# A gated MLP on one Trainium2 core: seven-product up tiles for 28 of 44 tiles, with part of VectorE's work moved to GpSimd

## The chip, the core and the metric

The kernel runs on one core of a Trainium2 chip. The core has TensorE (PE; its weight loads are shown as PEld), VectorE (DVE), ScalarE (ACT), GpSimd (POOL) and SyncE (SP), which issues DMAs here. The metric is the device time of one execution in microseconds (us); less is better.

## What is computed

One layer of an encoder in float32: attention in two head groups, an output projection, and a gated MLP with a convolution of width 3 over the positions of the gate branch. The change concerns the MLP:

```
def conv_glu(x, w_gate, w_up, conv_w, conv_b, w_down):
    g = x @ w_gate
    u = x @ w_up
    pad = CONV_W // 2
    gp = jnp.pad(g, ((0, 0), (pad, pad), (0, 0)))
    gc = conv_b
    for i in range(CONV_W):
        gc = gc + conv_w[i] * gp[:, i:i + L]
    return (jax.nn.silu(gc) * u) @ w_down
```

The model width is 2048 (16 blocks of 128 rows, `KC`), the hidden width 5632 (44 tiles of 128, `FC`), and 256 positions count at the end; 258 are carried where the convolution needs its neighbours.

## The kernel before

*Numbers in two parts.* TensorE multiplies in a reduced float32 form (`fp32r`). To keep precision every operand is split: a high part `whi` (ScalarE's copy into that form) and a low part `wlo = raw - whi` (VectorE's subtraction). A product then takes three matmuls (high by high, high by low, low by high). Each weight that is loaded (`raw`) therefore costs a ScalarE and a VectorE instruction over all its columns: `split_hi`, `split_lo`, line L251 (ScalarE) and L255 (VectorE's two-operand instructions). There are four `whi` and four `wlo` buffers, so at most four pieces of 1024 columns stand ready or in use.

*Kinds of tile.* A **gate tile** is 16 blocks of three matmuls over 258 columns (`mm3`, L734 to L736), an ordinary **up tile** 16 blocks of one matmul over 512 columns (high by both parts of x) and one over 256 (`mm2`, L2056 and L2057). Four up tiles that form a **quad** are done another way, by a scheme with seven products of 2 x 2 blocks in place of eight (`RowPair`, `scheme_products`, L291): for each of 8 pairs of row blocks, 7 products of three matmuls over 256 columns. It needs sums of the four weight quarters (`weight_sums`: one VectorE instruction over 512 columns and two over 256, each of which uses the result of the one before), which are split like weights, and sums `S` of the blocks of x, which lie ready in `near` buffers (or are loaded). So a pair has 1792 columns to split and not 1024. At a quad's end `quad_out` and `seven` combine the products (7 VectorE instructions that read a PSUM bank), eight transposes on TensorE (L297) turn the result, and `quad_value` multiplies it by the gate.

*The gate branch.* `gated` scales the product, `convolved` applies the three taps: the first on ScalarE (L251), the second and the third on VectorE (L263), then ScalarE's silu. `finish_value` splits the product of gate and up tile into `act`, and `pair_sums`/`value_sums` make, for every two tiles, the sums that the down products need: four VectorE instructions over 128 columns, then two splits (`split_plain`).

*Order.* `QUADS = (4, 10, 16, 22, 28)` names each quad's first tile. The list `work` is the order of pieces on TensorE: for each quad its 16 pieces are interleaved with those of the gate tiles (and of the ordinary gate and up tiles up to the next quad). From tile 34 on the rest is mixed with the products of the down projection. The queues of all engines are written out beforehand by a planner (`Flow`): every instruction is a `yield` of an engine and a cost in ns, the planner picks the one that can start first, and each engine then runs its list in that order. `ACT`, `TT` and `STT` (VectorE), `PTT` (GpSimd, L279) and `MM` are such helpers. `made` is the pool of buffers for weight sums; in the MLP it holds one (`more_raw`) until later buffers join it. `near_to(g)` says for how many quads the sums `S` of pair g stay in an `act` buffer that its values do not need yet; `ev_far` tells when it is free.

Of the kernel before, what the change touches and what calls it, by code (L numbers as in the profile page):

```python
# [9 lines left out]
F32 = mybir.dt.float32  # L10
F32R = mybir.dt.float32r
# [4 lines left out]
P = 128  # L16
# [30 lines left out]
ST = SF // P  # L47
SL = 1024
SM = SF - SL
QUADS = (4, 10, 16, 22, 28)  # L50
MID = 34


def near_to(g):

    return sum(f <= FC - KC + 2 * g for f in (*QUADS, MID)[1:])


# [160 lines left out]
def encoder_block(ctx: ExitStack, tc: tile.TileContext, io):  # L219
# [57 lines left out]
    def PTT(out, a, b, op):  # L277
        yield "pool", 90 + (2.7 if fl.cur.t < 4e5 else 3.9) * size(out)
        nc.gpsimd.tensor_tensor(out, a, b, op)  # L279

    def cost(l, r):
        n, m = size(r), l.shape[-1]
        if r.dtype != F32R:
            return max(1.69 * n, 3.33 * m, 50)
        return 0.445 * n + 3 if n >= 256 else max(0.84 * n, 0.84 * m, 27)

    def MM(items):

# [193 lines left out]
    for w, f in enumerate(QUADS):  # L482

        g, end = f // 2, (*QUADS, MID)[w + 1] // 2
        rest = tile_pair("gate", g) + tile_pair("gate", g + 1)
        for i in range(g + 2, end):
            rest += tile_pair("gate", i) + tile_pair("up", i)
        scheme = []
        for i in range(KC // 2):
            r = RowPair(io["w_up_s"][w][i], i, PW // 4, "up")  # L490
            r.first, r.last, r.quad = i == 0, i == KC // 2 - 1, f
            r.near = w < near_to(i)
            r.last_near = w + 1 == near_to(i)
            scheme += [(p, "scheme", r, 0) for p in r.pieces]
        lead, tail = 3, 2
        middle = rest[lead : len(rest) - tail]
        work += rest[:lead]
        for i, u in enumerate(scheme):
            a, b = (j * len(middle) // len(scheme) for j in (i, i + 1))
            work += [u] + middle[a:b]  # L500
        work += rest[len(rest) - tail :]
# [127 lines left out]
    def weight_sums(r):  # L629
        yield r.loaded  # L630
        q = r.q
        if r.wide:
            if r.mode == "both":
                yield r.summed[0]
                r.at["more"] = yield from one(made)
            else:
                yield r.first_loaded
                r.at["two"], r.at["more"] = yield made, 2
            low, up, t, m = (r.at[k] for k in ("lower", "upper", "two", "more"))
            if r.mode == "both":  # L640
# [12 lines left out]
            return  # L653
        t = r.at["sums"] = yield from one(made)
        raw = r.at["raw"]
        if r.mode == "third":
            yield from TT(t[:, :q], raw[:, :q], raw[:, q : 2 * q], ALU.add)
            yield from TT(t[:, q : 2 * q], t[:, :q], raw[:, 3 * q :], ALU.add)
            yield from TT(t[:, 2 * q : 3 * q], t[:, :q], raw[:, 2 * q : 3 * q], ALU.subtract)
            fl.set(r.summed[0])  # L660
        else:
            yield from TT(t[:, : 2 * q], raw[:, q : 3 * q], raw[:, : 2 * q], ALU.add)
            fl.set(r.summed[0])
            yield from TT(t[:, 2 * q : 3 * q], raw[:, 2 * q : 3 * q], t[:, :q], ALU.add)
            yield from TT(t[:, 3 * q :], t[:, 2 * q : 3 * q], raw[:, 3 * q :], ALU.add)
        fl.set(r.summed[1])
        r.used("raw")

# [61 lines left out]

    def mm3(ps, xhi, xlo, start, stop):
        whi, wlo = yield from block()
        yield "pe", 3 * (0.445 * size(xhi) + 3)
        nc.tensor.matmul(ps, whi, xhi, start=start, stop=False)  # L734
        nc.tensor.matmul(ps, whi, xlo, start=False, stop=False)  # L735
        nc.tensor.matmul(ps, wlo, xhi, start=False, stop=stop)  # L736
        used()
# [416 lines left out]
    sum_b = apool.tile([P, NT], F32, name="sum_b")  # L1154
    ev_sum_a, ev_sum_b = Event(), Event()

    def split_plain(hi, lo, src):
        yield from ACT(hi, src, AF.Copy)
        yield from TT(lo, src, hi.bitcast(F32), ALU.subtract)

# [736 lines left out]
    def mlp_buffers():  # L1897

        nonlocal act, mts, mpool
        yield ev_s2t  # L1900
        yield ev_resT
        actx.close()
        mpool = ctx.enter_context(tc.tile_pool(name="mpool", bufs=1))
        act = mpool.tile([P, FC, 2, SEQ], F32R, name="act")
        mt_rows[:] = tiles(mpool, 3, [P, 4 * NT], "mt")
        mts = Slots([t[:, i * NT : (i + 1) * NT] for t in mt_rows for i in range(4)])
        for t in tiles(mpool, 2, [P, PW], "sin"):
            fl.put(s_parts, t)
        for t in tiles(mpool, 1, [P, PW], "more_raw"):
            fl.put(made, t)  # L1910
        for b in banks[4:]:
            fl.put(acc, b)
        for i in range(KC // 2):
            f = FC - KC + 2 * i
            near[i] = act[:, f : f + 2].rearrange("p f i t -> p (f i t)").bitcast(F32)
        fl.set(ev_mlp)
        for i, (dst, saved) in enumerate(saved_sums["up"][:EARLY]):
            yield saved
            yield "sp", 600
            load(near[i], dst, ev_near[i], nc.sync)  # L1920
# [12 lines left out]
    def convolved(f, gs):  # L1933
        gc = yield from one(mts)
        g_ = gc[:, :SEQ]
        yield from ACT(
            g_, gs[:, 1 : 1 + SEQ], AF.Identity, scale=vec("conv0", f), bias=vec("conv_b", f)
        )
        yield from STT(g_, gs[:, :SEQ], vec("conv1", f), g_, ALU.mult, ALU.add)
        yield from STT(  # L1940
            gc[:, 1:SEQ], gs[:, : SEQ - 1], vec("conv2", f), gc[:, 1:SEQ], ALU.mult, ALU.add
        )
        yield from ACT(gs[:, :SEQ], g_, AF.Silu)
        fl.put(mts, gc)
        gates[f] = gs
        fl.set(ev_gate[f])
# [11 lines left out]
    def finish_value(f, u):  # L1958
        fl.put(mts, gates[f])
        u_ = u[:, :SEQ]  # L1960
        if f >= FC - KC:
            yield ev_far[(f - FC + KC) // 2]
        yield from ACT(act[:, f, 0, :], u_, AF.Copy)
        yield from TT(act[:, f, 1, :], u_, act[:, f, 0, :].bitcast(F32), ALU.subtract)
# [12 lines left out]
    def value_sums(dst, saved, a, b, place=None):  # L1977

        (A11, A21), (A12, A22) = ((t[:, :P], t[:, P:SEQ]) for t in (a, b))

# [71 lines left out]
    def mm2(ps, x, n, start, stop):  # L2052

        whi, wlo = yield from block()
        yield "pe", 347
        nc.tensor.matmul(ps, whi, x, start=start, stop=False)  # L2056
        nc.tensor.matmul(ps[:, :n], wlo, x[:, 0, :], start=False, stop=stop)  # L2057
        used()
# [4 lines left out]
    def mlp_weights():  # L2063
        pss, f = [], 0
        for p, kind, which, q in work:
# [15 lines left out]
            else:  # L2081
                if f == 0:
                    ps = yield from one(acc)
                for _ in range(p.n // P):
                    yield ev_act[f]
                    if which < KC - ST - 1:
                        yield from mm2(ps, act[:, f], SEQ, f == 0, f == FC - 1)
                    else:
                        yield from mm3(
                            ps[:, :SEQ], act[:, f, 0, :], act[:, f, 1, :], f == 0, f == FC - 1  # L2090
                        )
                    f += 1
                if f == FC:
# [29 lines left out]
    def scheme_products(p, r):  # L2123
# [5 lines left out]
        for i, n in enumerate(p.products):  # L2129
            if r.first:  # L2130
                yield from sums7_bank(r, n)
            if n in (1, 2, 4):
                k, h = {1: (0, 0), 2: (1, 0), 4: (1, 1)}[n]
                k += 2 * r.g
                A = hl[k] if r.of == "up" else act[:, k]
                a = [A[:, j, h * P : (h + 1) * P] for j in range(2)]
            else:
                yield r.ev_S
# [16 lines left out]
        if p is r.pieces[-1]:  # L2155
# [14 lines left out]
            if r.last:  # L2170
# [301 lines left out]
```

## Time and profile before

| | |
|---|---|
| runs | 1103.39, 1103.25, 1102.38 us; median 1103.25 |
| span of the profiled execution | 1102.0 us |
| its own time beside the span | the page gives no other; the span is 1.25 us under the median |
| TensorE, VectorE, ScalarE, GpSimd busy | 99%, 92%, 68%, 11% of the span |
| granted TensorE clock | 0.999 |
| attention and output projection | from 0 to about 400 us, the last of it beside the first gate tiles |
| gate and up tiles | from about 390 to 921 us |
| rest of the down products | to the end |

In the profile, a line of a group reads: source line, engine, operation, output<-inputs, partitions x elements and type, count | busy us, mean ns | idle us of the engine just before, and what ended it. In an order of time: start us, us from the start to the end, engine and instruction, count when alike ones are merged. Instructions of one engine overlap a little, so the distance of two starts says more than a duration.

### The profile page before, as it was taken

The page shows a single profiled execution, that of the slowest core. Times are in us where ns is not written, and L with a number is a line of the kernel's source. Part 1 is how long each engine was busy: PE and PEld are TensorE (multiplying, and loading weights), DVE is VectorE, ACT ScalarE, POOL GpSimd, SP SyncE. Part 2 cuts the span into 40 slices and gives each one's busy share as a digit, 9 for nine tenths or more (in the row PEclk, how much of TensorE's full clock was granted, in tenths as well). Part 3 has the DMA queues.
Part 4 walks back from the last instruction along what each step waited for, and adds up shares of the span by engine and source line. Part 5 has one row for each costly group of instructions (what it writes and reads, how often), then busy time and mean ns, then how long its engine had stood idle before and what let it go on. Part 6 is the DMA issues. An engine that isn't in the chain of part 4 may idle for free.

```text
span 1102.0 us, 22408 instructions
## 1 busy us (share of the span) xinstructions
PE 1094.0 (99%) x8164; PEld 1046.5 (95%) x8164; DVE 1015.0 (92%) x1935; ACT 751.1 (68%) x1507; POOL 120.8 (11%) x199
## 2 busy tenths in 40 slices
PE   9999999999999999999999999999999999999998
PEld 9999999999999999999999999999999999888887
DVE  8969887988878989999999999999999989999997
ACT  8688978888646776656666666665666656566663
POOL 3211222232443400000000000000000000000001
PEclk9999999999999999999999999999999999999999
DMA  9765678567877778655666656758788878699891
GB/s 327 253 230 176 197 218 236 149 203 182 255 207 208 229 256 324 215 193 192 224 221 209 225 192 237 262 193 285 264 299 287 292 237 322 205 320 336 302 331 45
DMA packets 82166, 262.72 MB, mean 238 GB/s; under 512 B 9224, under 2 KB 13320, under 8 KB 82056
## 3 DMA queue, kind: packets, MB, share of 16 engines
q1 hardware_dynamic: 78600, 252.38, 66.0%
q0 software_dynamic: 3168, 8.65, 5.2%
q8 instruction: 64, 1.05, 0.4%
q14 instruction: 46, 0.38, 0.1%
q10 hardware_dynamic: 288, 0.27, 0.1%
HBM read 243.82 MB, written 34.08 MB: 252 GB/s over the span
## 4 chain that ended last, share of the span: by engine, by line
PE 87%; ACT 5%; DVE 4%; DMA 2%; issue 1%; SPq 0%; POOL 0%; DVEq 0%; ACTq 0%; POOLq 0%
PE bank L291 27%; PE bank L734 14%; PE bank L735 14%; PE bank L736 14%; PE bank L2056 11%; PE bank L2057 6%; PE bank L297 2%; ACT whi L251 1%; DVE wlo L255 1%; DVE scr L263 1%; ACT scr L251 1%; DMA scr<-scr 1%; ACT qraw L251 0%; DMA early<-in_w_down_s 0%; DMA raw<-in_w_cq 0%
## 5 line engine op out<-in xcount | busy, mean ns | idle before, releaser
L251 ACT ACTIVATE whi<-raw 128x512 fp32r<-128x512 f32 (+2 forms) x493 | 354.1, 738 | 158.5 <-PE bank L735 54.6
L255 DVE TENSOR_TENSOR wlo<-raw,whi 128x512 fp32r<-128x512 f32 (+2 forms) x493 | 408.0, 848 | 30.7 <-ACT whi L251 29.8
L734 PE MATMUL bank<-hl,whi 128*128 128x258 f32 (+1 forms) x1208 | 347.8, 288 | 0.1
L735 PE MATMUL bank<-hl,whi 128*128 128x258 f32 (+1 forms) x1208 | 343.7, 285 | 0.0
L736 PE MATMUL bank<-hl,wlo 128*128 128x258 f32 (+1 forms) x1208 | 343.1, 284 | 0.2 <-DVE wlo L255 0.2
L736 PEld LDWEIGHTS bank<-hl,wlo 128*128 128x128 f32 x1208 | 229.7, 190 | 0.6 <-DVE wlo L255 0.4
L735 PEld LDWEIGHTS bank<-hl,whi 128*128 128x128 f32 x1208 | 229.3, 190 | 0.1
L734 PEld LDWEIGHTS bank<-hl,whi 128*128 128x128 f32 x1208 | 228.2, 189 | 0.8 <-ACT scr L251 0.3
L291 PE MATMUL bank<-whi,act 128*128 128x256 f32 (+1 forms) x574 | 143.5, 302 | 0.0
L2056 PE MATMUL bank<-hl,whi 128*128 128x512 f32 x384 | 136.6, 395 | 0.0
L2057 PE MATMUL bank<-hl,wlo 128*128 128x256 f32 x384 | 107.7, 280 | 0.0
L291 PEld LDWEIGHTS bank<-whi,act 128*128 128x128 f32 x574 | 100.2, 189 | 5.2
L251 ACT ACTIVATE whi<-more_raw 128x1024 fp32r<-128x1024 f32 x69 | 71.8, 1040 | 42.7 <-DVE more_raw L255 22.7
L291 PE MATMUL bank<-wlo,act 128*128 128x256 f32 (+1 forms) x287 | 86.8, 302 | 0.0
L2056 PEld LDWEIGHTS bank<-hl,whi 128*128 128x128 f32 x384 | 72.1, 188 | 14.9
L255 DVE TENSOR_TENSOR wlo<-more_raw,whi 128x1024 fp32r<-128x1024 f32 x69 | 82.6, 1196 | 3.2 <-ACT whi L251 3.1
L279 POOL TENSOR_TENSOR halves<-halves,resT 128x256 f32<-128x256 f32 x4 | 3.0, 784 | 703.9 <-ACT halves L251 703.9
L2057 PEld LDWEIGHTS bank<-hl,wlo 128*128 128x128 f32 x384 | 72.4, 188 | 0.0
L291 PE MATMUL bank<-whi,sin 128*128 128x256 f32 (+1 forms) x248 | 69.0, 325 | 0.0
L251 ACT ACTIVATE whi<-halves 128x1024 fp32r<-128x1024 f32 (+2 forms) x57 | 52.2, 936 | 22.4 <-PE bank L291 7.5
L255 DVE TENSOR_TENSOR wlo<-halves,whi 128x1024 fp32r<-128x1024 f32 (+2 forms) x57 | 60.4, 1074 | 0.5 <-ACT whi L251 0.3
L291 PEld LDWEIGHTS bank<-wlo,act 128*128 128x128 f32 x287 | 54.3, 189 | 2.2
(323 smaller groups left out, 2216.1 us busy)
## 6 DMA issues: line engine op xcount, KB each, us to landing
raw<-in_w_gate SPq DMA_DIRECT2D x88, 512.0 KB, 5.1
raw<-in_w_in SPq DMA_DIRECT2D x52, 512.0 KB, 4.5
raw<-in_w_up SPq DMA_DIRECT2D x48, 512.0 KB, 4.5
raw<-in_w_up_s SPq DMA_DIRECT2D x40, 512.0 KB, 4.4
raw<-in_w_out SPq DMA_DIRECT2D x32, 512.0 KB, 5.1
sin<-s_down SPq DMA_DIRECT2D x28, 512.0 KB, 6.5
raw<-in_w_down_m SPq DMA_DIRECT2D x21, 512.0 KB, 5.4
s_down<-sums SPq DMA_DIRECT2D x20, 512.0 KB, 6.5
```

What stands on the lines that cost most here:

```text
L251: nc.scalar.activation(out, in_, f, **kw)
L255: nc.vector.tensor_tensor(out, a, b, op)
L263: nc.vector.scalar_tensor_tensor(out, a, s, b, op0, op1)
L279: nc.gpsimd.tensor_tensor(out, a, b, op)
L291: nc.tensor.matmul(o, l, r, start=start, stop=stop)
L297: nc.tensor.transpose(o, i, ident[:n, :n])
L734: nc.tensor.matmul(ps, whi, xhi, start=start, stop=False)
L735: nc.tensor.matmul(ps, whi, xlo, start=False, stop=False)
L736: nc.tensor.matmul(ps, wlo, xhi, start=False, stop=stop)
L2056: nc.tensor.matmul(ps, whi, x, start=start, stop=False)
L2057: nc.tensor.matmul(ps[:, :n], wlo, x[:, 0, :], start=False, stop=stop)
```

## The change

Quads start every four tiles (seven of them); between two quads there are then no ordinary gate and up tiles, and only after the last quad do two follow. In `weight_sums` the two 256-wide sums go to GpSimd for the up weights. In `convolved` the third tap is ScalarE's product and GpSimd's addition. In `pair_sums` the two low parts are GpSimd's for the first 18 of 22 pairs. The sums `S` of pair 2 no longer lie in `act`: they are loaded for each quad, and the 4 KB a partition so saved are a second buffer for weight sums (`more_sums`) until the last quad, then the values of tiles 32 and 33 (`act_two`). The planner's TensorE costs change from `0.445 * n + 3` to `stream(n)`, and the pieces ahead and behind in a quad's order from 3 and 2 to 2 and 1.

```
-QUADS = (4, 10, 16, 22, 28)
+QUADS = (4, 8, 12, 16, 20, 24, 28)
...
+SUMS_IN = 2
 def near_to(g):
+    if g == SUMS_IN:
+        return 0
     return sum(f <= FC - KC + 2 * g for f in (*QUADS, MID)[1:])
...
+    def stream(n):
+        return n / 2.4 + 0.436 * -(-n // 16) + 4.7
...
-        return 0.445 * n + 3 if n >= 256 else max(0.84 * n, 0.84 * m, 27)
+        return stream(n) if n >= 256 else max(0.84 * n, 0.84 * m, 27)
...
-        lead, tail = 3, 2
+        lead, tail = 2, 1
...
             yield from TT(t[:, : 2 * q], raw[:, q : 3 * q], raw[:, : 2 * q], ALU.add)
             fl.set(r.summed[0])
-            yield from TT(t[:, 2 * q : 3 * q], raw[:, 2 * q : 3 * q], t[:, :q], ALU.add)
-            yield from TT(t[:, 3 * q :], t[:, 2 * q : 3 * q], raw[:, 3 * q :], ALU.add)
+            op = PTT if r.of == "up" else TT
+            yield from op(t[:, 2 * q : 3 * q], raw[:, 2 * q : 3 * q], t[:, :q], ALU.add)
+            yield from op(t[:, 3 * q :], t[:, 2 * q : 3 * q], raw[:, 3 * q :], ALU.add)
...
-        yield "pe", 3 * (0.445 * size(xhi) + 3)
+        yield "pe", 3 * stream(size(xhi))
...
-    def split_plain(hi, lo, src):
+    def split_plain(hi, lo, src, TT=TT):
...
-        act = mpool.tile([P, FC, 2, SEQ], F32R, name="act")
+        tile_of = mpool.tile([P, FC - 2, 2, SEQ], F32R, name="act")
+        f = FC - KC + 2 * SUMS_IN
+        act = [tile_of[:, i - 2 * (i > f)] for i in range(FC)]
...
+        near[SUMS_IN] = mpool.tile([P, PW], F32, tag="act_two", name="more_sums")
+        fl.put(made, near[SUMS_IN])
...
-        yield from STT(
-            gc[:, 1:SEQ], gs[:, : SEQ - 1], vec("conv2", f), gc[:, 1:SEQ], ALU.mult, ALU.add
-        )
+        yield from ACT(gs[:, : SEQ - 1], gs[:, : SEQ - 1], AF.Copy, scale=vec("conv2", f))
+        yield from PTT(gc[:, 1:SEQ], gc[:, 1:SEQ], gs[:, : SEQ - 1], ALU.add)
...
-        yield from value_sums(*saved_sums["down"][g], *(t[:, :SEQ] for t in pair))
+        op = PTT if g < LAST - 3 else TT
+        yield from value_sums(*saved_sums["down"][g], *(t[:, :SEQ] for t in pair), TT=op)
...
-            yield from split_plain(hl_[:, i], hl_[:, 2 + i], t)
+            yield from split_plain(hl_[:, i], hl_[:, 2 + i], t, TT)
...
-        yield "pe", 347
+        yield "pe", stream(2 * SEQ) + stream(SEQ)
...
                     fl.spawn(quad_out(r.quad, r.order, P7, dict(sum_banks)))
+                    if r.quad == QUADS[-1]:
+                        fl.spawn(sums_out())
+
+    def sums_out():
+        for t in (yield made, 2):
+            if t is not near[SUMS_IN]:
+                fl.put(made, t)
+        f = FC - KC + 2 * SUMS_IN
+        t = mpool.tile([P, 2, 2, SEQ], F32R, tag="act_two", name="act_two")
+        act[f : f + 2] = [t[:, i] for i in range(2)]
+        fl.set(ev_far[SUMS_IN])
```

More of the change, by code (lines that the diff above doesn't have):

```diff
@@ L1914, in mlp_buffers @@
             f = FC - KC + 2 * i
-            near[i] = act[:, f : f + 2].rearrange("p f i t -> p (f i t)").bitcast(F32)
+            t = tile_of[:, f - 2 * (i > SUMS_IN) :][:, :2]
+            near[i] = t.rearrange("p f i t -> p (f i t)").bitcast(F32)
+        near[SUMS_IN] = mpool.tile([P, PW], F32, tag="act_two", name="more_sums")
+        fl.put(made, near[SUMS_IN])
         fl.set(ev_mlp)
         for i, (dst, saved) in enumerate(saved_sums["up"][:EARLY]):
+            if i == SUMS_IN:
+                continue
             yield saved
@@ L1962, in finish_value @@
             yield ev_far[(f - FC + KC) // 2]
-        yield from ACT(act[:, f, 0, :], u_, AF.Copy)
-        yield from TT(act[:, f, 1, :], u_, act[:, f, 0, :].bitcast(F32), ALU.subtract)
+        yield from ACT(act[f][:, 0, :], u_, AF.Copy)
+        yield from TT(act[f][:, 1, :], u_, act[f][:, 0, :].bitcast(F32), ALU.subtract)
         fl.set(ev_act[f])
@@ L1976, in encoder_block, with value_sums @@
     values, last_S = {}, {g: ([], Event()) for g in (LAST - 1, LAST)}
-    def value_sums(dst, saved, a, b, place=None):
+    def value_sums(dst, saved, a, b, place=None, TT=TT):
         (A11, A21), (A12, A22) = ((t[:, :P], t[:, P:SEQ]) for t in (a, b))
@@ L2086, in mlp_weights @@
                     if which < KC - ST - 1:
-                        yield from mm2(ps, act[:, f], SEQ, f == 0, f == FC - 1)
+                        yield from mm2(ps, act[f], SEQ, f == 0, f == FC - 1)
                     else:
                         yield from mm3(
-                            ps[:, :SEQ], act[:, f, 0, :], act[:, f, 1, :], f == 0, f == FC - 1
+                            ps[:, :SEQ], act[f][:, 0, :], act[f][:, 1, :], f == 0, f == FC - 1
                         )
@@ L2134, in scheme_products @@
                 k += 2 * r.g
-                A = hl[k] if r.of == "up" else act[:, k]
+                A = hl[k] if r.of == "up" else act[k]
                 a = [A[:, j, h * P : (h + 1) * P] for j in range(2)]
```

## The prediction

> **What bounds the kernel now.** I read the page's engine shares first, and VectorE's line of the slices (tenths of 40 equal slices):
>
> ```profile
> PE 1094.0 (99%) x8164; PEld 1046.5 (95%) x8164; DVE 1015.0 (92%) x1935; ACT 751.1 (68%) x1507; POOL 120.8 (11%) x199
> DVE  8969887988878989999999999999999989999997
> ```
>
> TensorE is busy nearly all the time, VectorE too from the middle on. The view by stretches says the same of the gated MLP, and that GpSimd does nothing there, where the up tiles are made (columns PE, PEld, DVE, ACT, POOL busy, clock, DMA share, GB/s):
>
> ```profile
> 500.00:800.00 300.00, 300.00 (x2364) 292.99 (x2363) 294.62 (x546) 191.77 (x301) 0.00 (x0) 1.00 0.66 228
> ```
>
> Busy time of a pipelined engine says little, so I go by start times. First the chain of work that ended last: one pair of row blocks of a quad is 21 products, and the eight transposes mark each quad's end.
>
> ```profile
> 511.93 2.48 PE bank L291 x21
> ...
> 558.29 0.87 PE bank L297 x8
> ...
> 624.95 0.87 PE bank L297 x8
> ```
>
> Quads follow each other every 66.66 us (624.95 - 558.29). The order of time on TensorE gives the price of the other two kinds of tile:
>
> ```profile
> 519.77 0.28 PE L735 MATMUL bank<-hl,whi 128*128 128x258 f32 x1
> ...
> 521.46 0.28 PE L291 MATMUL bank<-whi,act 128*128 128x256 f32 x1
> ...
> 559.71 0.40 PE L2056 MATMUL bank<-hl,whi 128*128 128x512 f32 x1
> 560.06 0.39 PE L2056 MATMUL bank<-hl,whi 128*128 128x512 f32 x1
> ```
>
> From 519.77 to 521.46 there start 14 matmuls of 258 columns, 0.1207 us each: a gate tile (48 of them) is 5.79 us. A block of an ordinary up tile takes 0.35 (560.06 - 559.71), a tile of 16 blocks 5.6. Eight pairs (8 x 2.48 = 19.8), the transposes (0.87), six gate tiles (34.7) and two up tiles (11.2) make 66.6: the period is TensorE's own work without a hole. So a saving in matmuls would count in full, as long as VectorE follows. How near VectorE is, its order of time shows:
>
> ```profile
> 518.90 1.22 DVE L255 TENSOR_TENSOR wlo<-more_raw,whi 128x1024 fp32r<-128x1024 f32 x1
> 520.04 0.28 DVE L255 TENSOR_TENSOR mt<-mt 128x128 f32<-128x128 f32 x1
> 520.24 0.69 DVE L255 TENSOR_TENSOR more_raw<-raw 128x512 f32<-128x512 f32 x1
> ...
> 521.76 2.15 DVE L255 TENSOR_TENSOR wlo<-raw,whi 128x1024 fp32r<-128x1024 f32 x3
> 523.83 0.42 DVE L255 TENSOR_TENSOR sums<-mt,sums 128x256 fp32r<-128x256 f32 x1
> 524.17 0.28 DVE L255 TENSOR_TENSOR mt<-mt 128x128 f32<-128x128 f32 x1
> ```
>
> By starts, an instruction of 1024 takes 1.14 us, one of 256 0.34, one of 128 0.20; the three low parts of a pair and a gate piece's share (1024 + 512 + 256) 2.07. One of 512 lasts 0.69 and overlaps its successor by some 0.08, so 0.60; a tap 0.40 (0.48 in the groups, less the same overlap). Counted by the code, VectorE's period of six tiles is: low parts of the pairs 8 x 2.07 = 16.6, weight sums 8 x (0.60 + 0.34 + 0.34) = 10.2, 16 plain pieces 18.2, 33 instructions of 256 for 11.2, 12 taps 4.8, 12 of 128 for 2.4: 63.4 of 66.66 us, 95%. Two engines are at their limit together, and VectorE has 3 us to give.
>
> **The change, part by part.** *Two more quads.* Each takes four up tiles (4 x 5.6 = 22.4) off TensorE and adds 19.8 + 0.87: 1.7 us, 3.4 for both. The load bytes are equal; S of pair 2 is loaded once per quad, half a megabyte in 44 us beside 228 GB/s, hidden. The buffer that held it serves as a second place for the weight sums.
>
> *The period gets shorter.* Quads 4 tiles apart hold four gate tiles and no ordinary up tile: 19.8 + 0.87 + 23.2 = 43.9 us of TensorE. There are six such periods; the last quad keeps one of six tiles. VectorE without the moved work needs: low parts 16.6, the first sums 8 x 0.60 = 4.8, 8 gate pieces 9.1, 19 of 256 (7 to combine the products, 4 gate evictions, 4 products with the gate, 4 low halves) 6.5, 4 taps 1.6, 8 of 128 1.6: 40.2 us, 92%. With that work left on VectorE it would be 40.2 + 20 x 0.34 + 4 x 0.40 = 48.6, over the 43.9. So the move is what the shorter period stands or falls with.
>
> *The move to GpSimd.* 24 instructions of 256 columns a period (16 weight sums, 4 taps, 4 low halves). While GpSimd idles through the MLP the trace before has no such row there; it has them in the attention stages, with the same kind of VectorE work beside them:
>
> ```profile
> 291.13 0.75 DVE L255 TENSOR_TENSOR scr<-bank,sum_b 128x258 f32<-128x258 f32 x2
> 291.80 1.12 DVE L255 TENSOR_TENSOR wlo<-raw,whi 128x512 fp32r<-128x512 f32 x1
> 292.84 0.47 DVE L263 SCALAR_TENSOR_TENSOR hl<-bank,vecs,hl 128x258 fp32r<-128x258 f32 x1
> ```
>
> ```profile
> 291.62 1.79 POOL L279 TENSOR_TENSOR res<-res,scr 128x258 f32<-128x258 f32 x2 [3.38 <-DVE scr L255]
> ```
>
> The low part that meets the first GpSimd instruction takes 1.12 us, not 0.68; the second GpSimd instruction ends at 293.41, 0.49 after that low part (292.92), although its forerunner had long ended. VectorE's next, with one operand in a PSUM bank, runs beside it at its usual 0.47. So the two engines shut each other out when VectorE reads two SBUF operands, and not when one is in a bank. How much that takes from VectorE in the mean, the groups of two stretches and of the MLP say (mean ns is the last number before the bar's idle time):
>
> ```profile
> L255 DVE TENSOR_TENSOR wlo<-raw,whi 128x512 fp32r<-128x512 f32 x33 | 27.5, 864 | 2.7 <-ACT whi L251 2.7
> L279 POOL TENSOR_TENSOR res<-res,scr 128x258 f32<-128x258 f32 x16 | 14.4, 920 | 26.5 <-DVE scr L255 26.5
> L279 POOL TENSOR_TENSOR sum_a<-sum_a,scr 128x258 f32<-128x258 f32 x2 | 1.9, 967 | 0.4 <-ACT scr L251 0.4
> ```
>
> ```profile
> L255 DVE TENSOR_TENSOR wlo<-raw,whi 128x512 fp32r<-128x512 f32 x22 | 15.5, 731 | 0.0
> L255 DVE TENSOR_TENSOR raw<-raw 128x128 f32<-128x128 f32 x16 | 9.0, 563 | 0.3
> L263 DVE SCALAR_TENSOR_TENSOR hl<-res,vecs,hl 128x258 fp32r<-128x258 f32 x16 | 8.7, 573 | 0.0
> L279 POOL TENSOR_TENSOR kr<-kr,scr 128x258 f32<-128x258 f32 x15 | 18.6, 1238 | 31.5 <-ACT scr L251 31.2
> ```
>
> ```profile
> L255 DVE TENSOR_TENSOR wlo<-raw,whi 128x512 fp32r<-128x512 f32 x36 | 24.6, 684 | 0.0
> L255 DVE TENSOR_TENSOR mt<-mt 128x128 f32<-128x128 f32 x61 | 17.1, 288 | 0.8
> L263 DVE SCALAR_TENSOR_TENSOR mt<-mt,vecs,mt 128x255 f32<-128x255 f32 x18 | 8.7, 484 | 0.5
> ```
>
> The first fence is of the stretch from 290 to 340, the second of 340 to 395, the third of 500 to 800. At 290 to 340, 33 low parts are 180 ns longer than undisturbed, 5.9 us for 18 GpSimd instructions: 0.33 each. At 340 to 395 it is 22 x 47 + 16 x 275 + 16 x 89 ns = 6.9 us for 15: 0.46. I take the middle, 0.40: the MLP has both the low parts of the first and the chained short ones of the second. Moved off VectorE: 0.34 to 0.40 each. The move is then worth nothing, and the period is VectorE's: 40.2 + 24 x 0.40 = 49.8 us against 43.9, 5.9 more, six times 35.4. There is a credit: the ring of split pieces is four deep, and before the change ScalarE waits mostly for TensorE to give a place back, so it runs full:
>
> ```profile
> L251 ACT ACTIVATE whi<-raw 128x1024 fp32r<-128x1024 f32 x73 | 77.3, 1059 | 62.2 <-PE bank L291 24.5 <-PE bank L2056 15.5 <-PE bank L735 10.2
> ```
>
> Three pieces ahead of 2.9 us each (8 x 3 x 0.1207) are 8.7 us that TensorE can eat once before it stalls; I take 5, since VectorE runs behind ScalarE.
>
> From both sides: the least the move can cost follows if every VectorE instruction with a bank operand falls beside GpSimd. Fifteen of the period's are such (5.1 us), so 35.1 us read SBUF twice, and GpSimd shuts them out for 24 x 0.49 = 11.8: 46.9, still 3.0 over 43.9. Six times 3.0, less the whole 8.7, is 9.3. The most by the rows is 0.46: 51.2, 7.3 over, 43.8 without credit.
>
> The Trainium skill (SBUF — State Buffer, section "SBUF: two separate sides") says that the pair of ports which both engines share is an exclusive lock held for a whole instruction, and that the loser waits in full. The trace agrees that one waits for the other, but what VectorE loses is 0.44 of GpSimd's 0.75 to 0.92 us; the sum goes by the 0.40.
>
> *The last period of six tiles.* VectorE: 63.4 less 16 x 0.34, 6 x 0.34 and 6 x 0.40, with 28 x 0.40 added: 64.7 under 66.66, no stall. Tiles 34 to 43 and 0 to 3 have a tap each and some of them the low halves, exchanged at about par (0.34 to 0.40 for 0.40).
>
> *ScalarE* gets the third tap's product (44 of 0.41 us) and 8 x 768 more columns of high parts per new quad; it is busy 191.77 of 300 us: hidden. Waits added: silu waits for GpSimd's sum, the second half of a pair's sums for two GpSimd instructions in a row (2.5 us at 1238 ns), and behind them queue the taps. A period has 24 x 1.24 = 30 us of GpSimd in 43.9, so it keeps up. The values of tiles 32 and 33 now wait until both places of the weight sums are handed back after the last quad; nothing reads them before the products with the down weights that come later, so 0. *The order of the queues* is planned anew with TensorE prices about 1% higher; in the attention stages, where VectorE has room, I put that at 0, within 2 us either way.
>
> *Sum.* -3.4 + 35.4 - 5 = +27 on the profiled span of 1102.0, which lies 1.25 under the median of the runs: 1103.25 + 27 = 1130.
>
> **Rivals.**
> *Faster: the exclusion is hidden.* Place: the 24 instructions of each short period. If VectorE loses less than (43.9 - 40.2) / 24 = 0.154 us to each, TensorE stays full and only the 3.4 us remain: 1100. For it: a pair of GpSimd instructions that cost VectorE nearly nothing, since they let it pass and ran beside evictions from banks:
>
> ```profile
> 381.89 0.75 DVE L255 TENSOR_TENSOR scr<-bank,sum_a 128x258 f32<-128x258 f32 x2
> ```
>
> ```profile
> 380.55 4.51 POOL L279 TENSOR_TENSOR kr<-kr,scr 128x258 f32<-128x258 f32 x2 [5.28 <-ACT scr L251]
> ```
>
> Against it: the shared time alone, 46.9 of 43.9.
>
> *GpSimd becomes the bound.* At the 2.25 us each of that last row (4.51 for two), 24 need 54 us a period, 10 over TensorE: 6 x 10 - 3.4 gives 1160. Against it: the means of 0.92 and 1.24.
>
> *The lock in full.* If, as the page quoted above has it, VectorE lost GpSimd's whole 0.75 us (what one undisturbed GpSimd instruction would hold; 0.92 is the mean row, waits included), the period is 40.2 + 24 x 0.75 = 58.2, 14.3 over: 6 x 14.3 - 3.4 gives 1186. Against it: the 0.44 lost at 291.80.
>
> *No change.* VectorE loses 0.18 to 0.20 each and the credit pays the rest: 1102 to 1104.
>
> **How the numbers follow.** The likeliest, VectorE as the bound in the short periods, has 0.68, with 1110 (the lower bound, 1103.25 - 3.4 + 9.3 = 1109) to 1143 (1103.25 - 3.4 + 43.8 = 1144) as its own range. GpSimd as the bound and the full lock together have 0.06, no change 0.05 and hidden 0.21. The range goes from 1099, so that the hidden case is in, to 1146. What a measurement of this kernel can tell from no change is about 0.2%, 2.2 us. Faster 0.21, same 0.05, slower 0.74.
>
> **What would show it.** Right: TensorE's busy share falls under 95% in the stretch of the quads, its waits name VectorE's low parts (L255), the transposes of quads stand about 49 us apart in six periods, the mean of the 1024-wide low parts rises well over 1219 ns, and GpSimd's new instructions take 0.9 to 1.6 us. Wrong: quads 44 us apart, TensorE still without holes, low parts near 1219. If quads are far apart while VectorE has idle time ended by GpSimd, GpSimd was the bound. The forecast fails if GpSimd gets its turns mostly beside bank evictions, or if VectorE's count of 40.2 is off by the 4 us of slack.

## The result, and the profile after

The changed kernel takes 1157.1 us (median of runs from 1154.29 to 1158.71) against 1103.35 beside it: a ratio of 1.0483, 95% interval 1.0467 to 1.0498. It is 53.8 us slower. The forecast was 1130 with a range up to 1146, so the sign was right and the size was not.

The page of the changed kernel, busy shares and slices:

```profile
PE 1112.0 (96%) x8260; PEld 1057.1 (92%) x8260; DVE 1046.1 (91%) x1757; ACT 776.8 (67%) x1577; POOL 379.3 (33%) x463
PE   9999999999999998999898889899999999999998
DVE  8879888888879889898998989898999999999997
POOL 3212223222434227384665647483530000000001
```

GpSimd's digits now run through the quads, and in some of those slices TensorE's fall to 8. By stretches (PE, PEld, DVE, ACT, POOL busy, clock, DMA share, GB/s):

```profile
500.00:600.00 100.00, 91.07 (x713) 88.35 (x713) 94.31 (x124) 61.53 (x102) 59.88 (x61) 0.97 0.59 195
600.00:700.00 100.00, 87.80 (x693) 84.84 (x692) 92.17 (x119) 58.12 (x99) 56.81 (x61) 0.98 0.60 194
```

The transposes that close a quad, as the view of their line shows them, before (L297, five quads) and after (L305, the first to the fifth quad). Eight of them a quad; the last two numbers ahead of the semicolon are the first and the last start:

```profile
L297 PE MATMUL bank<-ident,raw x40: 271/272/273, 491.5 to 758.9; 128*128 128x128 f32 x40
```

```profile
L305 PE MATMUL bank<-ident,raw x40: 270/273/329, 487.4 to 696.9; 128*128 128x128 f32 x40
```

The first and the last of a quad's eight transposes stand 0.8 us apart, so quads followed each other every (758.9 - 491.5 - 0.8) / 4 = 66.65 us before, and every (696.9 - 487.4 - 0.8) / 4 = 52.2 after, where TensorE's own work is 43.9. VectorE's and GpSimd's groups of the five short periods from 487 to 747:

```profile
L260 DVE TENSOR_TENSOR wlo<-raw,whi 128x1024 fp32r<-128x1024 f32 x40 | 57.3, 1442 | 13.3 <-ACT whi L256 13.3
L260 DVE TENSOR_TENSOR wlo<-raw,whi 128x512 fp32r<-128x512 f32 x40 | 34.0, 849 | 0.0
L260 DVE TENSOR_TENSOR wlo<-raw,whi 128x256 fp32r<-128x256 f32 x40 | 25.3, 633 | 0.0
L260 DVE TENSOR_TENSOR mt<-bank,mt 128x256 f32<-128x256 f32 x30 | 12.0, 413 | 0.2
```

```profile
L284 POOL TENSOR_TENSOR more_raw<-more_raw,raw 128x256 f32<-128x256 f32 x20 | 25.4, 1268 | 1.6
L284 POOL TENSOR_TENSOR mt<-mt 128x128 f32<-128x128 f32 x19 | 18.2, 957 | 1.6 <-DVE act L260 0.4
L284 POOL TENSOR_TENSOR mt<-mt,mt 128x128 f32<-128x128 f32 x21 | 17.9, 851 | 0.7
```

Low parts take 1442, 849 and 633 ns where they took 1219, 684 and 419; the form with a bank operand stays at 413 (418 before). This is the exclusion of the forecast. Two things in these rows were not in it: GpSimd also has 128-wide instructions (40 in the last two rows over five periods, eight a period), and VectorE is idle before low parts, waiting for ScalarE (13.3).

For the comparisons I summed VectorE's time between the transposes of successive quads from every instruction in the trace: its *work* (each instruction at the duration of its form undisturbed, less 0.08 of overlap), what instructions take *longer*, and the *idle* time of over 0.06 us. Means over the periods between the first and the fifth quad's end (in "narrow" the sixth's, with five quads the fourth's), in us. What a sum leaves out of the distance is small gaps: some 3 us where sums on VectorE use each other's results, about 1 otherwise.

| kernel | median | quads apart | VectorE: work | longer | idle |
|---|---|---|---|---|---|
| before (six tiles a period) | 1103.35 | 66.65 | 63.0 | 0.4 | 0.3 |
| changed | 1157.1 | 52.2 | 37.7 | 9.7 | 3.5 |
| changed, old prices | 1142.7 | 50.6 | 37.6 | 11.9 | 0.1 |
| changed, third tap first | 1149.4 | 50.9 | 38.0 | 10.8 | 1.3 |
| changed, narrow, old prices | 1100.5 | 43.7 | 38.0 | 0.4 | 4.4 |
| seven quads, all on VectorE, old prices | 1147.9 | 53.0 | 47.5 | 0.5 | 2.2 |
| seven quads, only weight sums moved, old prices | 1139.8 | 50.1 | 41.9 | 5.1 | 1.7 |
| five quads, all moved, old prices | 1109.4 | 67.8 | 50.4 | 12.2 | 4.2 |
| before with copies on GpSimd | 1184.9 | 82.4 | 62.6 | 10.7 | 6.0 |

### The profile page after: what moved, and what is told of

Read it like the earlier page. It is cut to its first block, busy times and chain, and to the rows that moved or that the text cites. A ratio compares the mean times of both kernels' runs of the same rounds, so it can differ in the third digit from the quotient of the medians.

```text
span 1155.3 us, 22793 instructions
## 1 busy us (share of the span) xinstructions
PE 1112.0 (96%) x8260; PEld 1057.1 (92%) x8260; DVE 1046.1 (91%) x1757; ACT 776.8 (67%) x1577; POOL 379.3 (33%) x463
## 3 DMA queue, kind: packets, MB, share of 16 engines
q8 instruction: 65, 1.06, 0.4%
## 4 chain that ended last, share of the span: by engine, by line
PE 60%; DVE 24%; ACT 6%; issue 5%; DMA 3%; POOL 1%; SPq 0%; DVEq 0%; ACTq 0%; POOLq 0%
PE bank L299 20%; DVE wlo L260 13%; PE bank L745 10%; PE bank L743 10%; PE bank L744 10%; PE bank L2072 6%; PE bank L2073 3%; ACT whi L256 3%; DVE mt L260 2%; PE bank L305 2%; DVE mt L268 1%; DMA scr<-scr 1%; DVE more_sums L260 1%; DVE act L260 1%; DVE more_raw L260 1%
## 5 line engine op out<-in xcount | busy, mean ns | idle before, releaser
L260 DVE TENSOR_TENSOR wlo<-raw,whi 128x512 fp32r<-128x512 f32 (+2 forms) x510 | 448.4, 902 | 53.2 <-ACT whi L256 49.7
L745 PEld LDWEIGHTS bank<-hl,wlo 128*128 128x128 f32 x1208 | 232.2, 192 | 21.2 <-DVE wlo L260 21.1
L743 PEld LDWEIGHTS bank<-hl,whi 128*128 128x128 f32 x1208 | 230.8, 191 | 7.8 <-ACT whi L256 6.7
L744 PEld LDWEIGHTS bank<-hl,whi 128*128 128x128 f32 x1208 | 231.9, 192 | 0.1
L284 POOL TENSOR_TENSOR mt<-mt,mt 128x255 f32<-128x255 f32 (+1 forms) x77 | 65.1, 849 | 133.7 <-ACT mt L256 124.4
L2072 PE MATMUL bank<-hl,whi 128*128 128x512 f32 x256 | 90.7, 393 | 0.0
L256 ACT ACTIVATE whi<-more_raw 128x1024 fp32r<-128x1024 f32 (+1 forms) x57 | 58.8, 1032 | 42.6 <-PE bank L299 13.3
L256 ACT ACTIVATE mt<-mt,vecs 128x256 f32<-128x256 f32 (+1 forms) x88 | 46.5, 549 | 51.1 <-DVE mt L268 27.4
L299 PE MATMUL bank<-whi,hl 128*128 128x256 f32 x336 | 78.1, 281 | 0.0
L260 DVE TENSOR_TENSOR wlo<-more_raw,whi 128x1024 fp32r<-128x1024 f32 (+1 forms) x57 | 73.2, 1284 | 3.8 <-ACT whi L256 3.6
L299 PEld LDWEIGHTS bank<-wlo,act 128*128 128x128 f32 x322 | 61.2, 190 | 13.1 <-DVE wlo L260 10.8
L2073 PE MATMUL bank<-hl,wlo 128*128 128x256 f32 x256 | 71.9, 281 | 0.4 <-DVE wlo L260 0.4
```

Of the source, the lines that this page charges most:

```text
L256: nc.scalar.activation(out, in_, f, **kw)
L260: nc.vector.tensor_tensor(out, a, b, op)
L299: nc.tensor.matmul(o, l, r, start=start, stop=stop)
```

## The experiments

Three theories stood for trial: (1) GpSimd and VectorE shut each other out; (2) the added waits and the planned order of the queues lose the time; (3) the planner's new prices lose it away from the moved work.

**Copies: exclusion without a user.** To the kernel before:

```
+    def again(a, b):
+        n = a.shape[-1]
+        yield from PTT(spare[0][:, :n], a, b, ALU.add)
...
             yield from TT(t[:, 3 * q :], t[:, 2 * q : 3 * q], raw[:, 3 * q :], ALU.add)
+            if r.of == "up":
+                fl.spawn(again(raw[:, 2 * q : 3 * q], t[:, :q]))
+                fl.spawn(again(t[:, 2 * q : 3 * q], raw[:, 3 * q :]))
```

and alike after the third tap and after the low halves of the value sums.

> The kernel before, five quads, VectorE doing all its work; GpSimd in addition repeats every weight sum of 256 columns, one addition per tap and the low halves of the value sums into a spare tile that nobody reads. No engine waits for a result of GpSimd. Theory 1 (exclusion: GpSimd and VectorE shut each other out of SBUF, some 0.3 us of VectorE per instruction): a period of six tiles has 28 such instructions, 63 + 28 x 0.3 = 71.4 us of VectorE against 66.7 of TensorE, so quads 71 to 74 us apart and 1125 to 1140 in all. Theory 2 (the loss of the changed kernel comes from waits for GpSimd's results): nothing waits for them here, quads stay 66.7 apart and the time 1103.

Measured: 1184.9 us, 1.0741 times the kernel before (1.0725 to 1.0757); quads 82 us apart. Its groups from 510 to 838:

```profile
L255 DVE TENSOR_TENSOR wlo<-raw,whi 128x512 fp32r<-128x512 f32 x32 | 27.6, 862 | 0.0
L255 DVE TENSOR_TENSOR more_raw<-more_raw,raw 128x256 f32<-128x256 f32 x32 | 24.7, 771 | 1.0
L255 DVE TENSOR_TENSOR more_raw<-raw,more_raw 128x256 f32<-128x256 f32 x31 | 14.5, 468 | 20.7 <-POOL spare L279 18.5
L255 DVE TENSOR_TENSOR mt<-bank,mt 128x256 f32<-128x256 f32 x32 | 12.0, 413 | 0.4
```

Nobody reads what GpSimd makes, and VectorE's instructions are 10.7 us longer a period: 0.38 for each of 28. So theory 1 is shown to act by itself. The number went past its 1140, though. The third row has most of the reason: VectorE sits 20.7 us, some 5 a period, until GpSimd has read a buffer that it wants to overwrite. I had said that nobody waits for GpSimd; a reader is waited for too.

**All on VectorE.** In the changed kernel:

```
-            op = PTT if r.of == "up" else TT
+            op = TT
...
-        yield from ACT(gs[:, : SEQ - 1], gs[:, : SEQ - 1], AF.Copy, scale=vec("conv2", f))
-        yield from PTT(gc[:, 1:SEQ], gc[:, 1:SEQ], gs[:, : SEQ - 1], ALU.add)
+        yield from STT(
+            gc[:, 1:SEQ], gs[:, : SEQ - 1], vec("conv2", f), gc[:, 1:SEQ], ALU.mult, ALU.add
+        )
...
-        op = PTT if g < LAST - 3 else TT
+        op = TT
```

> The changed kernel, seven quads, with the third tap, the weight sums and the value sums back on VectorE. VectorE's count for a short period is 48.6 us against 43.9 of TensorE. Theory 1 (exclusion ate what the move saved): quads 48 to 50 us apart, 1125 to 1135, that is 22 to 32 us faster than the changed kernel. Theory 2 (waits for GpSimd's results are the loss): the same direction. Theory 3 (the move did help, VectorE alone is worse): quads over 52 apart, 1160 or more.

Measured: 1155.6 us (ratio 1.047, 1.0455 to 1.0486), the same as the changed kernel's 1157.1. With these prices the move is worth nothing, which fits an exchange at par. But theory 1 had this kernel 22 to 32 us below the changed one, and theory 3 had it at 1160 or more, so no theory's number came. Both kernels lie some 25 us above my numbers, so something else was lost in both.

**Narrow: the same instructions, 16 columns each.** In the changed kernel, for the three moved kinds; the other columns of each sum are left out:

```
+    def NARROW(out, a, b, op):
+        yield "pool", 90 + 3.9 * size(out)
+        n = 16
+        nc.gpsimd.tensor_tensor(out[:, :n], a[:, :n], b[:, :n], op)
```

> The changed kernel with GpSimd's moved instructions cut to their first 16 columns (240 or 112 columns of each weight sum, tap and value sum are left out, the rest of the buffers holds old data). All instructions, waits and the order of the queues stay. Theory 1 (exclusion): VectorE's excess of some 10 us a short period goes, 38 us are left, TensorE is full again: quads 44 us apart, 1098 to 1106 in all, with what the attention stage lost left in. Theory 2 in its form that the planned order of the queues and the extra steps in the chains cost the time whatever they take: quads stay over 48 apart, over 1130.

Measured: 1110.2 us (ratio 1.0062, 1.0045 to 1.0078), quads 44 us apart, TensorE without holes in the quads. All waits and all instructions are there, only GpSimd's columns are not, and 47 of the 53.8 us are gone. That leaves the plain theory 2, an order that costs its time whatever the instructions take, nothing to explain in the quads. Narrow instructions are also shorter, so this run alone does not part the exclusion from GpSimd's latency; the copies, which nobody reads, and the column "longer" do. The time is 4 us above theory 1's range. The 10 us that remain over 1100 arise mostly ahead of the first quad's end, which the next runs look into.

**The new prices alone.** In the kernel before:

```
-        return 0.445 * n + 3 if n >= 256 else max(0.84 * n, 0.84 * m, 27)
+        return stream(n) if n >= 256 else max(0.84 * n, 0.84 * m, 27)
...
-        yield "pe", 3 * (0.445 * size(xhi) + 3)
+        yield "pe", 3 * stream(size(xhi))
...
-        yield "pe", 347
+        yield "pe", stream(2 * SEQ) + stream(SEQ)
```

> The kernel before with only the planner's TensorE costs changed to the new formula. The changed kernel's trace has 5.3 us more of TensorE holes in its first 400 us than before, where none of the moved work lies. Theory A (the new prices reorder the attention stage for the worse): 1107 to 1110. Theory B (the holes come from the changed MLP plan reaching back, or from the run): 1102 to 1105.

Measured: 1114.95 us (ratio 1.0105, 1.009 to 1.012), 11.6 us from a change that touches no instruction but only the order, 5 more than theory A's upper end. The longest waits of TensorE up to 500, before and with the new prices:

```profile
PE bank L291 <- POOL sq8r L279: 1.1, 3, 0.7
PE bank L866 <- DVE em L863: 1.1, 1, 1.1
PE bank L291 <- DVE late L255: 0.9, 1, 0.9
```

```profile
PE bank L739 <- DVE wlo L255: 2.0, 2, 1.5
PE bank L300 <- POOL p L279: 1.9, 4, 0.9
PE bank L294 <- POOL sq8r L279: 1.6, 4, 0.8
PE bank L294 <- DVE late L255: 1.5, 1, 1.5
```

There are more waits, and longer ones; most are for tiles that TensorE waited for before too, the one for GpSimd's `p` is new in the list. Measured by the distances of matmul starts, TensorE's holes grow by 5.9 us up to 400, 3.0 from 400 to 500, and 2.2 from 500 to 800.

**Prices up to 400 us only, and prices 1% lower.** Two variants of the kernel before: `stream` returns the old price from planned time 400 us on; and 0.440 in place of 0.445 (343 in place of 347 for a block of an ordinary up tile).

> The kernel before; the new TensorE prices hold only up to planned time 400 us, the old ones behind it. With them everywhere it took 1114.95: 5.9 us more of TensorE holes up to 400, 3.0 from 400 to 500, 2.2 from 500 to 800. Theory A (each stage's loss is its own order's): 1108 to 1111. Theory B (the holes up to 400 come back later, or the MLP's part is all that counts): 1103 to 1106.

> The kernel before with TensorE prices 1% lower than its own (0.440 for 0.445 a column), that is a step away from the new prices. Theory S (the loss grows with the price, since a planner that thinks TensorE slower starts the splits later): 1099 to 1104. Theory R (any other price reshuffles the queues, and the old one is a picked order): 1106 to 1116.

Measured: 1110.5 us (ratio 1.0067, 1.005 to 1.0084) and 1106.9 us (1.0034, 1.0021 to 1.0047). The first stage's loss is its own (theory A of the first). And it is no matter of more or less: a price 1% lower loses as well. All three changes of price that were tried lose, so the order of before is a good one among these neighbours, as theory R has it.

**The changed kernel with the old prices.**

```
-        return stream(n) if n >= 256 else max(0.84 * n, 0.84 * m, 27)
+        return 0.445 * n + 3 if n >= 256 else max(0.84 * n, 0.84 * m, 27)
```

and the same in `mm3` and `mm2`.

> The changed kernel with the planner's TensorE prices as before. The new prices alone cost the kernel before 11.7 us (1114.95): some 6 in the attention stages, the rest in the MLP. Theory A (that part is independent of the exclusion): the attention part comes back, the MLP part hides behind VectorE, 1148 to 1153. Theory B (the old prices make the MLP's queues fit too): 1140 to 1147.

Measured: 1142.7 us (ratio 1.0356, 1.0339 to 1.0373), 14.4 less than with the new prices: the MLP's queues fit too (theory B). VectorE's idle time in the quads is gone, and what is left is the exclusion. The end of the first quad, at 487.4 with the new prices, now comes at 480.3:

```profile
L305 PE MATMUL bank<-ident,raw x40: 270/273/318, 480.3 to 683.5; 128*128 128x128 f32 x40
```

```profile
L260 DVE TENSOR_TENSOR wlo<-raw,whi 128x1024 fp32r<-128x1024 f32 x40 | 58.9, 1491 | 0.0
L260 DVE TENSOR_TENSOR wlo<-raw,whi 128x512 fp32r<-128x512 f32 x40 | 40.8, 1021 | 0.0
L260 DVE TENSOR_TENSOR act<-mt,act 128x256 fp32r<-128x256 f32 x20 | 18.3, 952 | 0.0
```

The idle column is 0.0 in these rows; the low half of a value, 419 ns undisturbed, takes 952. Work 37.6 and 11.9 longer are 49.5 of the 50.6 us.

**Narrow with the old prices.**

> The changed kernel with GpSimd's moved instructions cut to 16 columns (the rest of those sums is left out) and the planner's old prices. If the two extra quads save the 3.4 us of matmuls that their count gives once VectorE has room, and the 10 us that the narrow variant still lost were the prices: 1098 to 1102. If something else of the change (S of pair 2, the later act buffer, the shorter lead) costs: over 1103.

Measured: 1100.5 us (ratio 0.9976, 0.9965 to 0.9987), 2.8 us less than before. Its groups from 480 to 732 and its transposes (six quads):

```profile
L260 DVE TENSOR_TENSOR wlo<-raw,whi 128x1024 fp32r<-128x1024 f32 x49 | 59.4, 1221 | 18.6 <-ACT whi L256 18.6
L260 DVE TENSOR_TENSOR wlo<-raw,whi 128x512 fp32r<-128x512 f32 x44 | 30.3, 688 | 1.2 <-ACT whi L256 1.1
...
L289 POOL TENSOR_TENSOR mt<-mt 128x16 f32<-128x16 f32 x46 | 22.9, 499 | 6.5 <-DVE act L260 2.9 <-ACT mt L256 1.6
```

```profile
L310 PE MATMUL bank<-ident,raw x48: 270/272/276, 473.4 to 692.6; 128*128 128x128 f32 x48
```

Quads are 43.7 us apart ((692.6 - 473.4 - 0.8) / 5), low parts take their undisturbed 1221 and 688. So the matmuls' saving is real, and nothing else in the change costs more than the 0.6 us by which it falls short of 3.4.

**Five quads with the move.** The changed kernel with `QUADS = (4, 10, 16, 22, 28)` and the old prices.

> The changed kernel with the five quads and the prices of before, so the move to GpSimd is nearly alone. Per period of six tiles VectorE keeps 51 of its 63 us and loses 40 instructions x 0.3 = 12 to the exclusion: 63 of 66.7. Theory 1 (the move exchanges at par): TensorE stays full, 1102 to 1106. Theory 2 (the queues' mutual waits that came with it, 3 us a period, count in full): quads 68 to 70 apart, 1110 to 1120.

Measured: 1109.4 us (ratio 1.0053, 1.0038 to 1.0068), quads 67.8 us apart: neither. VectorE's work falls from 63.0 to 50.4, its instructions take 12.2 longer: the exchange is at par within 1 us. But 4.2 us of idle time come with it, and these tip a period of 66.65. Most of that idle time ends with ScalarE's high parts (12.3 us over four periods, another 3.4 with loads). GpSimd's sums take 1.4 to 1.5 us each in the rows below, and ScalarE waits for its taps; that this is what delays the high parts is likely and was not tested.

```profile
L284 POOL TENSOR_TENSOR more_sums<-more_sums,raw 128x256 f32<-128x256 f32 x16 | 23.0, 1436 | 1.3
L284 POOL TENSOR_TENSOR more_raw<-raw,more_raw 128x256 f32<-128x256 f32 x15 | 22.9, 1530 | 17.1 <-DVE more_raw L260 17.1
```

**A planner that knows of the exclusion.** In the changed kernel:

```
         yield "pool", 90 + (2.7 if fl.cur.t < 4e5 else 3.9) * size(out)
+        if fl.cur.t >= 4e5:
+            fl.clock["dve"] += 300.0
         nc.gpsimd.tensor_tensor(out, a, b, op)
```

> The changed kernel; the planner adds 0.3 us to VectorE's clock for each GpSimd sum in the MLP, so the order of the queues is made for what the exclusion takes. Work and exclusion are the same. VectorE is idle 3 to 4 us in each short period of 51, mostly for ScalarE's high parts. Theory W (this idle time comes from an order planned without the exclusion): it goes, quads 48 to 49.5 apart, 1137 to 1147. Theory L (it is the latency of the chains, whatever the order): 1153 to 1160.

Measured: 1160.6 us (ratio 1.0519, 1.0504 to 1.0535): no gain, the idle time stays. Theory W, that the order is wrong because the planner does not know of the exclusion, falls. Theory L is not thereby shown: with the old prices, another order of the same chains, the idle time was gone.

**Seven quads with the old prices: all on VectorE, and only the weight sums moved.** The edits above (for the second only those of the tap and of the value sums), with the old prices.

> Seven quads, the moved work back on VectorE, the planner's prices of before. VectorE has 48.1 us of work a short period and some 2 us of gaps between sums that use each other's results: 50.1 against 43.9, six times 6.2 less 3.4. Theory 1 (the move exchanged VectorE's time at par): 1137 to 1145, the same within 5 us as the moved version with these prices (1142.7). Theory 3 (the move did relieve VectorE by more than it took): over 1150.

> Seven quads, prices of before, and of the moved work only the weight sums on GpSimd (16 instructions a short period); taps and value sums on VectorE. VectorE has 42.4 us, loses 16 x 0.38 = 6.1 to the exclusion and no longer has the gaps in the chain of sums: 48.5 to 49. Theory 1: 1125 to 1134, better than both all and nothing moved, since a sum moved also takes a gap in VectorE's chain with it. If a wide sum takes 0.5 from VectorE (the 0.49 seen for one instruction): 1136 to 1144.

Measured: 1147.9 us (ratio 1.0412, 1.0396 to 1.0427) and 1139.8 us (1.0334, 1.0318 to 1.0349). Both lie above what I expected of theory 1, the first by 3 us, the second by 6: I had left VectorE's idle 2 us a period out again. The second number does lie in the range for 0.5 us a wide sum, but by luck, since a sum took 0.32 (5.1 for 16). Moving all is worth 5 us against moving nothing, and moving only the sums 8; in the first pair the exchange itself loses (9.9 us less work, 11.4 longer), and what pays is that the idle time and the gaps between sums on VectorE go. As each of these kernels has an order of its own, and an order alone moved the time by as much, the few us between them are not shown to be the move's. Only the sums is the best use of GpSimd that was found, and it is 37 us behind the kernel before.

**The third tap first.** The changed kernel's product for the third tap overwrites the gate, so ScalarE must wait until VectorE has read it for the second tap. Given a place of its own it can go first:

```
-        gc = yield from one(mts)
+        gc, slot = yield mts, 2
...
+        third = slot[:, : SEQ - 1]
+        yield from ACT(third, gs[:, : SEQ - 1], AF.Copy, scale=vec("conv2", f))
...
-        yield from ACT(gs[:, : SEQ - 1], gs[:, : SEQ - 1], AF.Copy, scale=vec("conv2", f))
-        yield from PTT(gc[:, 1:SEQ], gc[:, 1:SEQ], gs[:, : SEQ - 1], ALU.add)
+        yield from PTT(gc[:, 1:SEQ], gc[:, 1:SEQ], third, ALU.add)
+        fl.put(mts, slot)
```

> The changed kernel; ScalarE makes the third tap's product before the second tap, into a place of its own, so it no longer waits for VectorE to have read the gate (in the changed kernel ScalarE waits 24.6 us for that from 450 to 750, and the high parts queue behind). Work and exclusion are the same. Theory H (this wait on ScalarE's queue is what leaves VectorE idle 3 to 4 us a short period): idle falls to about 1, quads 49 to 50 apart, 1143 to 1150. Theory P (the idle time comes with the new prices' order, whichever wait carries it): 1153 to 1160.

> The same with the planner's prices of before, where VectorE is idle less than half a microsecond a short period and only the exclusion is left (12 us of 50.4). Theory 1 (exclusion is the whole rest): the same as without the edit, 1140 to 1145. Theory H in full (the wait costs there too): 1130 to 1138.

Measured: 1149.4 us (ratio 1.0423, 1.0406 to 1.0441), 7.7 less than the changed kernel, with VectorE's idle time down from 3.5 to 1.3 us a period; with the old prices 1141.6 us (1.0355, 1.0339 to 1.037), no different from 1142.7. The two orders of time from the changed kernel show the wait (ScalarE, then VectorE; in brackets the idle time before and what ended it):

```profile
520.70 0.51 ACT L256 ACTIVATE mt<-mt,vecs 128x255 f32<-128x255 f32 x1 [2.77 <-DVE mt L268]
521.12 1.05 ACT L256 ACTIVATE whi<-raw 128x1024 fp32r<-128x1024 f32 x1
```

```profile
519.71 0.96 DVE L268 SCALAR_TENSOR_TENSOR mt<-mt,vecs,mt 128x256 f32<-128x256 f32 x1
522.20 1.42 DVE L260 TENSOR_TENSOR wlo<-raw,whi 128x1024 fp32r<-128x1024 f32 x1 [1.53 <-ACT whi L256]
```

VectorE's second tap comes late in its list and is itself held up by GpSimd (0.96 us, not 0.48), so ScalarE's product waits 2.77 us; the high part behind it in ScalarE's queue starts only at 521.12, and VectorE, done with the tap at 520.67, stands idle for 1.53 us until that is there. With the new prices theory H's time and idle time came, its distance of 49 to 50 us did not quite (50.9). From 450 to 750 VectorE waits 3.8 us for high parts where it waited 19.1. The edit also makes a new order of the queues, so that all 7.7 us are this wait's is likely and not shown. With the old prices, without the edit, ScalarE waits only 8.6 us for the second tap from 487 to 740, where it waits 21.5 with the new ones, and little is lost.

## Why the prediction was right and wrong, point by point

*The bound, and the two quads: right.* 43.9 us of TensorE a short period (43.7 measured without exclusion) and 3.4 us saved (2.8 measured).

*VectorE as the bound, at par: right in kind.* The move left 37.7 us of work where 40.2 was forecast, and instructions take 9.7 to 11.9 longer where 24 x 0.40 = 9.6 was. With the old prices the two make 49.5 where 49.8 was forecast, and that is luck, since the terms were counted wrongly in ways that nearly cancel: the new argument of `value_sums` is named `TT` and so shadows the helper inside it, and the four 128-wide instructions of every pair of tiles go to GpSimd as well. I read "the low halves" from the two calls and not from the whole function; the count is 32 instructions, at 0.30 (changed) to 0.37 (old prices) each.

*The step that failed: what was put at 0.* The order of the queues had no term in the sum, and ScalarE's new wait counted as hidden. Without the new order, with the planner's old prices, the changed kernel takes 1142.7 us, inside the range. In terms of the sum, from -3.4 + 35.4 - 5 = +27 to the measured +53.8:

- *The order of the queues "at 0, within 2 us"*: 14.4 us (1157.1 less 1142.7). Half of it is there when the first quad ends (487.4 against 480.3); most of that is the attention stages, where new prices cost the kernel before 5.9 us of TensorE holes, and 7.5 us in all with the prices up to 400 alone (1110.5). The other half comes in the five short periods that follow, in whose order VectorE idles 3.5 us a period. I treated a new plan as noise around the old one; it was the second largest term.
- *The added waits, "ScalarE: hidden".* ScalarE's busy share was right and beside the point. Its third-tap product waits for VectorE, and the forecast named the silu's wait but not this one, nor the high parts queued behind. The edit that takes it away gave 7.7 us back; this is part of the 14.4, since with the old prices the same edit gives nothing that can be told from no change.
- *The credit of 5 us from the ring*: not there. With the old prices the first short period already ends 6.9 us late (its transposes start at 480.3, against 473.4 with narrow instructions).
- *The exclusion itself*: 42.2 us (1142.7 less 1100.5) where 30.4 with the credit was forecast. Of the 11.8 between them 5 are the credit. Another 5 are the six short periods: at the sixth quad's end the kernel is 40.3 us behind the one with narrow instructions (732.1 against 691.8), 6.7 a period and not 5.9. The rest is in the last period, of six tiles, 0.7 longer than TensorE's 66.6, and behind it.

*The rivals.* "Hidden" needed under 0.154 us an instruction; it was 0.30 or more. The floor by shared time, 46.9 us a period, held. "GpSimd becomes the bound" did not come: it is busy 60 of 100 us. That its 1160 lies close to the measured 1157 is luck. The lock in full, by the Trainium skill's SBUF — State Buffer, section "SBUF: two separate sides", would have made 1186; VectorE lost 0.30 to 0.38 us in the mean to an instruction that undisturbed lasts 0.75, so the trace bears out the exclusion that the page states and not the full price that I worked out from it.

What stays open: why just this order makes VectorE and ScalarE wait for each other when another does not. The third tap's wait is perhaps half of it (7.7 of 14.4), the attention stages' 6 most of the rest; which lines of the plan carry those was not tried.

## What to carry to other kernels

Before work is moved to an engine that shuts out the one it relieves, price it by what the relieved engine's *other* instructions lose: a row of the same form with and without the neighbour is enough, and here it said "at par" before the change was run. Where lists of several engines are planned ahead, treat any change to the planner's prices as a change of its own, to be measured alone: some 1% in the prices of TensorE moved the kernel before by 4 to 12 us with every instruction the same. And of an added instruction count its wait and what queues behind it on its engine, not its duration.

## What the runs showed of the hardware that I had not expected

GpSimd instructions of 16 columns take nothing measurable from VectorE (low parts of 1221 ns beside them, 1219 without), though the profile gives them 0.37 to 0.66 us in six of their seven rows and 1.06 in the other. Those of 128 and 256 columns, 0.75 us undisturbed at 256, take 0.30 to 0.38 in the mean. So the loss does not go by the time that the profile gives for GpSimd; what one of 128 and one of 256 columns take was not measured apart.

The clock granted to TensorE fell below 1.00 in kernels in which TensorE stalls often: 0.97 in the changed kernel from 500 to 600, 0.975 over the whole run with the copies, and 0.981 with all seven quads on VectorE and old prices, where GpSimd does nothing in the quads; it was 1.00 in the narrow ones. It does not follow from the stalls alone: with the third tap first TensorE is busy only 88 of 100 us from 600 to 700, and the clock is 1.00. What the lower clock costs was not measured; TensorE had time to spare there.
